# Joint softmax of the attention groups in steps between gate products, and branch values loaded into the places of two gate operands

## The chip, the cores and the metric

The kernel runs on 1 core of a Trainium2 chip. The metric is the device time of one execution in microseconds (us). Before the change the median of 3 runs is 1984.87 us, between 1984.15 and 1985.83.

## The reference

One layer of a hybrid decoder on 1024 tokens of width 1024, all in fp32. Cut to what matters here:

```
z = rms_norm(x) @ W_in          # one projection, its columns shared by all that follows
y_a = rwkv7_mixer(z_a)  @ proj_a     # branch A, 512 wide
y_b = rglru_mixer(z_b)  @ proj_b     # branch B, 512 wide
for each of 3 groups g (dilation 1, 4, 8):     # branch C: attention, 4 heads of 64 in a group
    logits = q_g @ k_g + bias;  m = max(logits);  p = exp(logits - m);  l = sum(p)
    o_g = (p @ v_g) / l;        lse_g = m + log(l)
w = softmax over the groups of lse           # the joint softmax
y_c = (sum_g w_g * o_g) @ proj_c             # 256 wide
gates = sigmoid(z_gate)                      # 3 branches x 1024 columns
merged = gates_a * y_a + gates_b * y_b + gates_c * y_c
x = x + merged @ W_out
x = x + relu(rms_norm(x) @ W_up)^2 @ W_down
```

## The kernel before

**Products.** Each fp32 product runs on TensorE (PE) as three matmuls of split operands, `mm3` (L236 to L238): high by high, high by low, low by high. The high part is a cast on ScalarE (ACT), the low part a subtraction on VectorE (DVE) or GpSimd (POOL). `load_w` does this for weights (`wr_` raw, `wh_` and `wl_` the parts, L225 to L229), `load_y` for branch values (`yr` raw, `y...h` and `y...l`, L336 to L343). Raw tiles of both, and those of the gate columns (`wr_z`, L1270), share a tag `wraw` with two places of 512 KB: a third raw load waits until the cast and the subtraction of one before it have freed its place.

**Stages.** Norm; the recurrent branch B, whose values go to DRAM as `yb_d`; branch A (RWKV, `ya_d`) with the attention's value, query and key projections in its gaps; the attention with the gate products as filler; `gates`, which multiplies the branch values with `proj_b`, `proj_a`, `proj_c` and sums them under the gates; `tail` with W_out and the MLP. The change touches the stretch from the attention to the start of `gates`.

**Gate products** (`gate_z`, L1205 on) are a generator: each `next` emits one step. The gate columns form 12 pairs of 128-column blocks, four for each of the branches B, C, A in this order. Pairs 0 and 1 are multiplied directly. Each of the other ten is made by seven half-size products, here called by their right operand in the order B11, B21, T2, T1, T3, B22, T4 (product j = 0 to 6): 12 matmuls each into one of two PSUM banks. B11 to B22 are the four quarters of the normed input (`ht`, shown as `hh` and `hl` in the profile, pool `hp`); T1 to T4 are sums of them in pool `h2`, shown as `zT1h` and so on (T4 takes the places of B12 in `hp`). The results that an add completes (`th`, L1334 on DVE) free a bank: in the order listings `th_103` is the add for pair 10, product 3. A tanh (L1258, ACT) and a store to `th_d` follow. The seven left operands of the next pair, `wz`, come from two raw tiles; for j = 2 they take four sums on DVE (`wr_z`, `th_s`, L1285 to L1289). In the last pair, pair 11, step j = 1 calls `load_first`: the first projection weights, `wr_p10`, and the four loads of branch B's values (`yr10` to `yr13`) into `wraw`. Their parts go to the places of T2 and T1 in `h2`.

**Attention** (L974 on) works in six units (cc, g): cc is the half of the four heads, g the group; the order is (0,0), (0,1), (0,2), (1,0), (1,1), (1,2), counted n = 0 to 5. A unit loads query and key (`z0`, `z1`), its bias tile and the row of key norms spread over partitions (`rb`, L121, a tag with two places), and DVE scales the key by it (`z`, L1001). Then four steps sp, with two `tiles` yields each: scores (`l`, L1018) into PSUM, their scaling (`lg`, L1028, DVE, which frees the scores' bank), max, exponential on ACT, transposes (`pt`), and the weighted values (`o`, L1063, copied to `og` at L1162). In the order listings `lg0130` belongs to group 0, cc 1, sp 3, and `z1_11` is the key of unit (1,1). After each yield `filler` draws gate steps from the generator: 71 of its 86 are drawn here, the rest run behind the attention.

**Joint softmax.** After a unit, `combine_rows` transposes its maxima and sums (`stt` on PE L1072, `st` on DVE L1074), stores them (`st_d`) and loads them back as rows of 16 x 128 (`row`, L1080). `combine(cc)` then does the joint softmax of the three groups: maxima (L1092), differences (L1096), exponentials on ACT, denominators (L1101, L1103), a reciprocal, the weights (L1106), which go to DRAM (`cw_d`) and come back spread over 64 partitions each (`cb`, L121), and the weighted sum `yc` = cb x og (L1122) plus the two `yt` (L1126), added on POOL and stored to `yc_d` (L1128). `combine(0)` runs on POOL and is called at once at sp = 2 of unit n = 3. `combine(1)` runs on DVE and is called at once after the last unit. In the order listings `mx1`, `ct1`, `row001`, `cw11`, `cw21` are its small tiles.

**Order.** A scheduler that simulates a timeline at build time places the instructions; the order of the program text is its priority, and `issue_after` keeps a filler step behind the scores of an earlier step. On the chip each engine runs its list in order. All loads and stores of this stretch are issued by SyncE (SP), also in order: one that must wait holds those behind it.

## Time and profile before

| | |
|---|---|
| median of 3 runs | 1984.87 us |
| profiled execution | 1979.91 us, its span 1978.1 us |
| mean granted clock of PE | 0.988 |
| PE busy | 1906.3 us, 96% of the span |
| PE weight loads (overlap PE) | 1512.1 us |
| DVE busy | 1237.5 us, 63% |
| ACT, POOL busy | 763.5 and 774.5 us, 39% each |
| moved by DMA | 236.53 MB, mean 120 GB/s |
| stretch 800 to 1085 us (most of the attention) | PE busy 278.74 of 285 us |
| stretch 1085 to 1182 us (end of the attention, last gate pairs, start of `gates`) | PE busy 80.17 of 97 us |
| stretch 1182 us to the end | PE busy 786.09 of 796 us |

The times of all rows are in us from the start of the span. L numbers are lines of the kernel. In a row of the timeline an arrow in brackets gives how long the engine had stood before the instruction and what ended that. Rows of stretches give, behind the limits and the length, the busy time (and count) of PE, its weight loads, DVE, ACT and POOL, then the granted clock of PE, the share of the DMA engines and the GB/s. PE is the engine that is nearly always busy, so what counts is the time in which it stands and what it waits for.

### The profile page before, as it was taken

Reading aid. Unit: us, or ns where it says so; the run is one execution under the profiler, and the core shown is the slowest. Engines: PE = TensorE matmul, PEld = TensorE weight load, DVE = VectorE, ACT = ScalarE, POOL = GpSimd, SP = SyncE. Lnnn points to the kernel's source line nnn. Section 1 sums busy time; section 2 is a strip of 40 time slices with the busy share of each in tenths; the row PEclk is TensorE's granted clock in tenths of the full one; section 3 lists DMA queues with packets and bytes.
Section 4 is the critical chain, followed back from the end, with each engine's and each line's share of the span. In section 5 each row is a group of like instructions: output and inputs, shape, how many; then the busy total and the mean of one; then the engine's idle time right before and its main releaser. Section 6 shows DMA issues by size and latency. Waiting matters only on the chain.

```text
span 1978.1 us, 29765 instructions
## 1 busy us (share of the span) xinstructions
PE 1906.3 (96%) x11634; PEld 1512.1 (76%) x11634; DVE 1237.5 (63%) x1992; ACT 763.5 (39%) x1275; POOL 774.5 (39%) x631
## 2 busy tenths in 40 slices
PE   8999999999999999999999879998999999999999
PEld 6776777787677878777777658887888888888887
DVE  5556456656656564775454446446777567987875
ACT  5675223233323331455555331245323323333332
POOL 1343533442452340542533442244343343444542
PEclk9999999999999999999999999999999999999999
DMA  4122312221221221434443465552433439535231
GB/s 147 54 65 75 98 46 62 59 57 50 54 71 40 66 65 38 131 99 149 120 145 111 150 236 183 188 181 107 160 138 149 165 137 380 196 144 181 95 128 65
DMA packets 191618, 236.53 MB, mean 120 GB/s; under 512 B 38536, under 2 KB 133413, under 8 KB 191478
## 3 DMA queue, kind: packets, MB, share of 16 engines
q1 hardware_dynamic: 191302, 234.62, 35.9%
q8 instruction: 91, 1.49, 0.3%
q14 instruction: 49, 0.40, 0.1%
q0 software_dynamic: 160, 0.02, 0.0%
q10 hardware_dynamic: 16, 0.00, 0.0%
HBM read 168.14 MB, written 68.82 MB: 120 GB/s over the span
## 4 chain that ended last, share of the span: by engine, by line
PE 77%; DVE 8%; DMA 6%; ACT 3%; issue 3%; POOL 3%; SPq 1%; DVEq 0%; ACTq 0%; POOLq 0%
PE dx L236 3%; PE dx L237 3%; PE dx L238 3%; PE zg L236 3%; PE ux L236 3%; PE ux L237 3%; PE ux L238 3%; PE zg L237 3%; PE zg L238 3%; PE g_z L237 2%; PE g_z L236 2%; PE g_z L238 2%; PE wo L238 1%; PE wo L236 1%; PE dz L237 1%
## 5 line engine op out<-in xcount | busy, mean ns | idle before, releaser
L1482 POOL TENSOR_TENSOR wl_d<-dr,wh_d 128x1024 fp32r<-128x1024 f32 x40 | 101.0, 2525 | 127.5 <-ACT wh_d L1481 119.0
L1291 POOL TENSOR_TENSOR wz<-wr_z,wz 128x512 fp32r<-128x512 f32 x60 | 84.0, 1401 | 162.9 <-ACT wz L1290 137.9
L1482 DVE TENSOR_TENSOR du<-dq,du 128x1024 fp32r<-128x1024 f32 x56 | 124.1, 2216 | 23.6 <-ACT du L1481 22.9
L236 PE MATMUL dx<-wh_d,du 128*128 128x512 f32 x256 | 99.7, 389 | 0.4 <-DVE acc L1662 0.4
L237 PE MATMUL dx<-wl_d,du 128*128 128x512 f32 x256 | 99.6, 389 | 0.0
L238 PE MATMUL dx<-wh_d,du 128*128 128x512 f32 x256 | 99.4, 389 | 0.0
L1481 ACT CAST wh_d<-dr 128x1024 fp32r<-128x1024 f32 x40 | 42.1, 1053 | 142.0 <-PE dx L238 72.8
L777 DVE TENSOR_SCALAR s<-ac,wc 64x64 f32<-64x64 f32 x128 | 36.1, 282 | 73.4 <-PE ac L773 71.0
L237 PE MATMUL g_z<-hl,wh_z 128*128 128x512 f32 x192 | 77.4, 403 | 0.0
L1482 POOL TENSOR_TENSOR wl_a<-ur,wh_a 128x1024 fp32r<-128x1024 f32 x15 | 47.6, 3175 | 75.7 <-ACT wh_a L1481 75.7
L236 PE MATMUL g_z<-hh,wh_z 128*128 128x512 f32 x192 | 76.6, 399 | 0.4 <-DVE zsq L432 0.4
L238 PE MATMUL g_z<-hh,wl_z 128*128 128x512 f32 x192 | 77.0, 401 | 0.0
L1482 POOL TENSOR_TENSOR wl_s<-ur,wh_s 128x1024 fp32r<-128x1024 f32 x16 | 44.4, 2774 | 76.0 <-ACT wh_s L1481 76.0
L229 POOL TENSOR_TENSOR wl_wo<-wr_wo,wh_wo 128x1024 fp32r<-128x1024 f32 x16 | 38.6, 2413 | 62.7 <-ACT wh_wo L228 62.7
L1481 ACT CAST du<-dq 128x1024 fp32r<-128x1024 f32 x56 | 58.6, 1047 | 1.5 <-DMA dq<-u_d 1.5
L1662 DVE TENSOR_TENSOR acc<-dx,acc 128x512 f32<-128x512 f32 x64 | 42.0, 680 | 26.3 <-PE dx L238 26.3
L236 PE MATMUL v<-wh_wv,hh 128*128 128x256 f32 x192 | 56.4, 294 | 1.3 <-DVE st L783 1.3
L236 PEld LDWEIGHTS dx<-wh_d,du 128*128 128x128 f32 x256 | 48.0, 188 | 10.9 <-DVE acc L1662 0.9
L237 PEld LDWEIGHTS dx<-wl_d,du 128*128 128x128 f32 x256 | 48.0, 188 | 10.0
L238 PEld LDWEIGHTS dx<-wh_d,du 128*128 128x128 f32 x256 | 48.0, 188 | 9.9
L237 PE MATMUL v<-wl_wv,hh 128*128 128x256 f32 x192 | 55.6, 290 | 0.0
L238 PE MATMUL v<-wh_wv,hl 128*128 128x256 f32 x192 | 55.3, 288 | 0.0
(757 smaller groups left out, 6160.6 us busy)
## 6 DMA issues: line engine op xcount, KB each, us to landing
dq<-u_d SPq DMA_DIRECT2D x56, 512.0 KB
wr_z<-in_w_in_dram SPq DMA_DIRECT2D x32, 512.0 KB
ur<-in_mlp_up_dram SPq DMA_DIRECT2D x16, 1024.0 KB
dr<-in_mlp_down_dram SPq DMA_DIRECT2D x16, 1024.0 KB
th_d<-th SPq DMA_DIRECT2D x48, 256.0 KB
tg<-th_d SPq DMA_DIRECT2D x32, 256.0 KB
wr_wo<-in_w_out_dram SPq DMA_DIRECT2D x16, 512.0 KB
qk_d<-zo SPq DMA_DIRECT2D x24, 256.0 KB
```

The lines of the kernel that those rows point to most:

```text
L229: E.tensor_tensor(lo, raw, hi, ALU.subtract)
L236: PE.matmul(ps, lh, rh, start=first and i == 0, stop=False, skip_group_check=skip)
L237: PE.matmul(ps, lh, rl, start=False, stop=False, skip_group_check=skip)
L238: end = PE.matmul(ps, ll, rh, start=False, stop=last and i == n - 1, skip_group_check=skip)
L777: V.tensor_scalar(ns[half[h], :], pb[h][half[h], 128 * j + 64 * c : 128 * j + 64 * c + 64], wc[half[h], 2 * i + c : 2 * i + c + 1], None, ...
L1291: (V if i == 2 else G).tensor_tensor(l, src, h, ALU.subtract)
L1481: A.copy(hi, src)
L1482: split.last = E.tensor_tensor(lo, src, hi, ALU.subtract)
L1662: V.tensor_tensor(acc[row][:, half[col]], ps, acc[row][:, half[col]], ALU.add)
```

## The change

Three things change.

1. `combine` becomes a generator with eleven yields: after the maxima, the exponentials, the denominators, the weights (two), and each of the six products with `og`. `combine(0)` starts at sp = 0 of unit n = 3 and takes two steps at each yield of the tiles that follow; what is left runs at the end of the unit. `combine(1)` still starts after the last unit, with one gate step drawn between its steps.
2. The raw values of branches B and A no longer pass through `wraw`. `raws` takes the places of B11 (for yb) and of B21 (for ya), high and low tile of each, as two tiles of 128 x 2 x 1024, and `load_first` issues the four loads of 1 MB: `yr1h` and `yr1l` hold rows 0 to 255 and 256 to 511 of `yb_d`, `yr0h` and `yr0l` those of `ya_d`. `load_y` with `raw` splits from there. The values of branch C (`yc`) still pass through `wraw`.
3. `load_first` is defined and handed over before `attention` is called, since more of the gate steps now run inside it, and the pool `yp` is opened behind the attention.

```
-    attention(..., fill)
...
-    def load_y(src, b, ks, place):
+    def load_y(src, b, ks, place, raw=None):
         for k in ks:
-            r = wp.tile([P, T], F32, tag="wraw", name=f"yr{b}{k}", bufs=2)
-            S.dma_start(r, src[k * P : (k + 1) * P, :])
+            r = (raw or (lambda k: wp.tile([P, T], F32, tag="wraw", name=f"yr{b}{k}", bufs=2)))(k)
+            if raw is None:
+                S.dma_start(r, src[k * P : (k + 1) * P, :])
             h, l = (place(k, x) for x in "hl")
             A.copy(h, r)
             (G if k % 2 else V).tensor_tensor(l, r, h, ALU.subtract)
...
+    def raws(b, kh):
+        t = []
+        for x in "hl":
+            r = hp.tile([P, 2, T], F32, tag=f"h{x}{kh}0", name=f"yr{b}{x}")
+            t += [r[:, 0], r[:, 1]]
+            S.dma_start(r, (yb_d if b else ya_d)[256 * "hl".index(x) : 256 * "hl".index(x) + 256, :].rearrange("(k p) t -> p k t", p=P))
+        return lambda k: t[k]
...
     def load_first():
         late.append(load_w(io["proj_b"][0][:, 0:256]...))
-        load_y(yb_d, 1, range(4), in_block(("T2", "T1"), 1))
+        late.extend((raws(1, 0), raws(0, 1)))
+        load_y(yb_d, 1, range(4), in_block(("T2", "T1"), 1), late[2])
     late.append(load_first)
+    attention(..., fill)
...
     def load_ya():
-        load_y(ya_d, 0, range(2), in_block(("T3",), 0))
-        load_y(ya_d, 0, range(2, 4), in_yp(0))
+        load_y(ya_d, 0, range(2), in_block(("T3",), 0), late[3])
+        load_y(ya_d, 0, range(2, 4), in_yp(0), late[3])
...
         def combine(cc):
...                                   # maxima
+            yield
...                                   # differences, exponentials
+            yield
...                                   # denominators, reciprocal
+            yield
...                                   # weights, cw_d, for cc = 1 the spread cb
+            yield
+            yield
             for hf in range(2):
                 for g, dil in enumerate(DILS):
...                                   # one product of cb and og
+                    yield
                 S.dma_start(yc_d[...], y)
...
+        sums = iter(())
...
                 for i, _ in enumerate(tiles(cc, g, sp, po)):
                     filler(0.2 if i else 2)
+                    next(sums, None)
+                    next(sums, None)
...
-                if sp == 2 and n == 3:
-                    combine(0)
+                if sp == 0 and n == 3:
+                    sums = combine(0)
+            for _ in sums:
+                pass
             combine_rows(cc, g)
-        combine(1)
+        for _ in combine(1):
+            filler(1)
```

**First place: DVE where unit (1,0) ends and the key of unit (1,1) is scaled.** `z1_11` waits for `rb`, the two `lg013` pairs free the scores of unit (1,0)'s last step, `th_6x` are gate adds. The rows carry each kernel's own line numbers: L1001, L1028 and L1334 became L1012, L1039 and L1357. Before:

```order
L1334 TENSOR_TENSOR th_63_9705<-zg60_9529,th_63_9705 128x512
L1001 SCALAR_TENSOR_TENSOR z1_11_9740<-z1_11_9740,der_111,rb110_9744 128x512
L1028 SCALAR_TENSOR_TENSOR lg0130_9660<-l0130_9654,sst_84,bias01_9237 128x256 x2
L1334 TENSOR_TENSOR th_62_9688<-zg61_9530,th_62_9688 128x512
L1001 SCALAR_TENSOR_TENSOR z1_11_9740<-z1_11_9740,der_111,rb111_9748 128x512
L1031 TENSOR_REDUCE stat01_9247<-lg0130_9660 128x2
L1028 SCALAR_TENSOR_TENSOR lg0131_9668<-l0131_9655,sst_84,bias01_9237 128x256 x2
```

After:

```order
L1039 SCALAR_TENSOR_TENSOR lg0131_9649<-l0131_9636,sst_84,bias01_9237 128x256 x2
L1309 TENSOR_TENSOR wr_z71_9574<-wr_z71_9574 128x512
L1042 TENSOR_REDUCE stat01_9247<-lg0131_9649 128x2
L1046 TENSOR_SCALAR nm0131_9650<-stat01_9247 128x2
L1311 TENSOR_TENSOR th_s7_9691<-wr_z70_9572,wr_z71_9574 128x512
L1312 TENSOR_TENSOR wr_z70_9572<-wr_z70_9572,th_s7_9691 128x512
L1314 TENSOR_TENSOR wz72_9688<-th_s7_9691,wz72_9688 128x512
L1357 TENSOR_TENSOR th_63_9686<-zg60_9553,th_63_9686 128x512
L1357 TENSOR_TENSOR th_62_9669<-zg61_9554,th_62_9669 128x512
L1012 SCALAR_TENSOR_TENSOR z1_11_9740<-z1_11_9740,der_111,rb110_9744 128x512
L1085 COPY st3201_9809<-stt01_9807 32x128
L1182 COPY og01_9318<-o013_9634 128x256
```

Both pairs of `lg013` now stand ahead of the two `z1_11` (that of `lg0130` five rows above the first row shown), and the gate adds `th_63` and `th_62` too; the `st` of unit (1,0) and a copy of the last `og01` come in between the first `z1_11` and the second, which is the row behind the last one shown.

**Second place: DVE behind the last `st`, with the arithmetic of `combine(1)` behind it.** Before, from the gate add that stands ahead of the arithmetic:

```order
L1334 TENSOR_TENSOR th_100_10670<-zg101_10657,th_100_10670 128x512
L1092 TENSOR_TENSOR mx1_10582<-mx1_10582,row201_10576 16x128
L1285 TENSOR_TENSOR wr_z110_10675<-wr_z111_10677,wr_z110_10675 128x512
L1096 TENSOR_TENSOR row001_9812<-row001_9812,mx1_10582 16x128
L1096 TENSOR_TENSOR cw11_10588<-row101_10258,mx1_10582 16x128
```

and from the last row of the arithmetic, fourteen rows further down:

```order
L1106 TENSOR_TENSOR cw21_10591<-cw21_10591,mx1_10582 16x128
L1334 TENSOR_TENSOR th_103_10726<-zg100_10656,th_103_10726 128x512
L1334 TENSOR_TENSOR th_102_10709<-zg101_10657,th_102_10709 128x512
L1122 TENSOR_TENSOR yc10_10615<-cb10_10602,og01_9318 128x512
L1126 TENSOR_TENSOR yt101_10617<-cb11_10607,og11_9818 128x512
L1126 TENSOR_TENSOR yt102_10620<-cb12_10612,og21_10264 128x512
L1126 TENSOR_TENSOR yt111_10626<-cb11_10607,og11_9818 128x512
L1126 TENSOR_TENSOR yt112_10629<-cb12_10612,og21_10264 128x512
L1334 TENSOR_TENSOR th_110_10804<-zg110_10790,th_110_10804 128x512
```

After, from the end of the arithmetic:

```order
L1120 TENSOR_TENSOR cw21_10609<-cw21_10609,mx1_10582 16x128
L1357 TENSOR_TENSOR th_100_10626<-zg101_10613,th_100_10626 128x512
L1308 TENSOR_TENSOR wr_z110_10631<-wr_z111_10633,wr_z110_10631 128x512
L1309 TENSOR_TENSOR wr_z111_10633<-wr_z111_10633 128x512
L1138 TENSOR_TENSOR yc10_10713<-cb10_10661,og01_9318 128x512
L1311 TENSOR_TENSOR th_s11_10708<-wr_z110_10631,wr_z111_10633 128x512
L1312 TENSOR_TENSOR wr_z110_10631<-wr_z110_10631,th_s11_10708 128x512
L1142 TENSOR_TENSOR yt101_10733<-cb11_10666,og11_9818 128x512
L1314 TENSOR_TENSOR wz112_10705<-th_s11_10708,wz112_10705 128x512
L1357 TENSOR_TENSOR th_103_10703<-zg100_10612,th_103_10703 128x512
L1142 TENSOR_TENSOR yt102_10754<-cb12_10671,og21_10264 128x512
L1142 TENSOR_TENSOR yt111_10797<-cb11_10666,og11_9818 128x512
```

Before, the add `th_100` stood ahead of the arithmetic and the sums for `wz112` were spread through it, with the four `yt` in one piece behind `th_102`. Now `th_100` and the four sums stand behind the arithmetic, and `th_103` and `th_102` between the products with `og`.

**Third place: SP around the loads of the branch values.** `wr_p10` and `wr_p00` are the first projection weights of branches B and A, `tb` the gate values that `gates` reads back. Before:

```order
L1259 DMA th_d_80<-th_103_10726 128x512
L1259 DMA th_d_80<-th_102_10709 128x512
L1259 DMA th_d_80<-th_106_10784 128x512
L225 DMA wr_p10_10824<-in_proj_b_dram 128x4x256
L1128 DMA yc_d_71<-yc10_10615 128x512
L340 DMA yr10_10830<-yb_d_70 128x1024
L1259 DMA th_d_80<-th_110_10804 128x512
L340 DMA yr11_10836<-yb_d_70 128x1024
L340 DMA yr12_10840<-yb_d_70 128x1024
L1128 DMA yc_d_71<-yc11_10624 128x512
L1259 DMA th_d_80<-th_113_10876 128x512
L1372 DMA tb100_10935<-th_d_80 128x512
```

After:

```order
L1282 DMA th_d_80<-th_103_10703 128x512
L1145 DMA yc_d_71<-yc10_10713 128x512
L1282 DMA th_d_80<-th_102_10686 128x512
L1282 DMA th_d_80<-th_106_10769 128x512
L360 DMA yr1l_10823<-yb_d_70 128x2x1024
L360 DMA yr1h_10821<-yb_d_70 128x2x1024
L225 DMA wr_p10_10815<-in_proj_b_dram 128x4x256
L1145 DMA yc_d_71<-yc11_10776 128x512
L360 DMA yr0l_10827<-ya_d_69 128x2x1024
L360 DMA yr0h_10825<-ya_d_69 128x2x1024
L225 DMA wr_p00_10995<-in_proj_a_dram 128x4x256
L1282 DMA th_d_80<-th_110_10792 128x512
```

The two loads of branch B's values stand ahead of its weights, and those of branch A follow ahead of every read of `tb`; the stores of `yc` keep their places on either side of branch B's loads.

More of the change, by code (lines that the diff above doesn't have):

```diff
@@ L330, in hybrid_block @@
     fill = gate_z(tc, w_in, ht, h2, hp, gt, wp, pg, th_d, load_cols, mm3, late)
-    attention(tc, io, dbg, psum, der, cg, yc_d, bias_d, sst, rk_d, cw_d, v_d, qk_d, fill)
-    yp_p = tc.tile_pool(name="yp", bufs=1)
-    yp = yp_p.__enter__()
     ys = {}
-    def load_y(src, b, ks, place):
+    def load_y(src, b, ks, place, raw=None):
         for k in ks:
-            r = wp.tile([P, T], F32, tag="wraw", name=f"yr{b}{k}", bufs=2)
-            S.dma_start(r, src[k * P : (k + 1) * P, :])
+            r = (raw or (lambda k: wp.tile([P, T], F32, tag="wraw", name=f"yr{b}{k}", bufs=2)))(k)
+            if raw is None:
+                S.dma_start(r, src[k * P : (k + 1) * P, :])
             h, l = (place(k, x) for x in "hl")
@@ L358, in load_first @@
         late.append(load_w(io["proj_b"][0][:, 0:256].rearrange("(k p) c -> p k c", p=P), [P, 4, 256], "p10"))
-        load_y(yb_d, 1, range(4), in_block(("T2", "T1"), 1))
+        late.extend((raws(1, 0), raws(0, 1)))
+        load_y(yb_d, 1, range(4), in_block(("T2", "T1"), 1), late[2])
     late.append(load_first)
+    attention(tc, io, dbg, psum, der, cg, yc_d, bias_d, sst, rk_d, cw_d, v_d, qk_d, fill)
+    yp_p = tc.tile_pool(name="yp", bufs=1)
+    yp = yp_p.__enter__()
     for _ in fill:
```

## The prediction

> **What bounds the kernel now.** I read the page first, then the waits of PE between 800 and 1260 us, then stretches of time, then the timelines of PE and DVE and the chain of waits where PE stood.
>
> ```profile
> span 1978.1 us, 29765 instructions
> PE 1906.3 (96%) x11634; PEld 1512.1 (76%) x11634; DVE 1237.5 (63%) x1992; ACT 763.5 (39%) x1275; POOL 774.5 (39%) x631
> ```
>
> PE is busy in 96% of the span and no matmul is removed, so only PE's own standing can be won: at most 72 us, most of it in stages that the change leaves alone. The waits of PE in the stretch that it touches (in total, times, longest):
>
> ```profile
> PE zg L236 <- DVE th L1334: 7.4, 3, 4.9
> PE l L1018 <- DVE lg L1028: 4.8, 3, 2.4
> PE pj L236 <- ACT y0T3h L342: 4.5, 1, 4.5
> PE pj L236 <- ACT y20h L342: 2.4, 1, 2.4
> PE pj L236 <- ACT wh_p L228: 1.4, 2, 1.0
> PE pj L237 <- POOL y1T1l L343: 1.3, 1, 1.3
> PE pj L237 <- DVE y20l L343: 0.5, 1, 0.5
> ```
>
> ```profile
> 1085.00:1182.00 97.00, 80.17 (x337) 61.79 (x334) 42.94 (x58) 32.60 (x48) 41.64 (x23) 0.96 0.58 188
> ```
>
> Between 1085 and 1182 us PE stands 16.8 us (97.00 less 80.17), and its granted clock is 0.96 there. PE's timeline places the waits for th and lg:
>
> ```profile
> 986.97 1.09 PE L1063 MATMUL o<-ptS,vt 128*64 128x128 f32 x16
> 1002.75 0.92 PE L1018 MATMUL l<-z,z 64*128 64x128 f32 x4 [2.45 <-DVE lg L1028]
> 1109.30 0.50 PE L236 MATMUL zg<-zT4h,wz 128*128 128x512 f32 x1 [1.76 <-DVE th L1334]
> 1112.18 0.39 PE L236 MATMUL zg<-hh,wz 128*128 128x512 f32 x1
> 1120.11 0.39 PE L238 MATMUL zg<-zT2h,wz 128*128 128x512 f32 x1
> 1125.40 0.79 PE L236 MATMUL zg<-zT1h,wz 128*128 128x512 f32 x1 [4.90 <-DVE th L1334]
> ```
>
> From 1112.18 to 1120.11 there are 36 matmuls, so one takes 7.93/35 = 0.227 us and a gate product of 12 takes 2.72.
>
> **The change part by part.** *Attention unit (1,1).* The wait of 2.45 is a queue on DVE:
>
> ```profile
> 1000.91 0.99 DVE L1001 SCALAR_TENSOR_TENSOR z<-z,der,rb 128x512 f32<-128x512 f32 x1 [5.32 <-DMA rb<-rk_d]
> 1001.83 0.86 DVE L1028 SCALAR_TENSOR_TENSOR lg<-l,sst,bias 128x256 f32<-128x256 f32 x2
> ```
>
> DVE stood 5.32 us for rb with the lg of the last tiles behind it, and those hold the score banks. In the new order (first place in the change section) both lg pairs stand ahead of that z. PE reaches the first scores of the unit after 57 gate matmuls from the o at 986.97 instead of 53, and eight pt, eight o and one stt more: 988.1 + 57 x 0.227 + about 2.3 (1.1 for the o by the row at 986.97, as much for the pt by estimate) is 1003.3. The z can be done by 1001.9, as now. So the 2.45 goes. Bounds: 0 gained if rb comes that much later (a bias load and a th_d store now stand ahead of it on SP), 2.45 if not; I take 2.45, since the z has over a microsecond to spare.
>
> *The joint softmax of the second half*, combine(1). DVE now:
>
> ```profile
> 1093.15 0.28 DVE L1074 COPY st<-stt 32x128 f32<-32x128 f32 x1 [5.86 <-PE stt L1072]
> 1093.73 0.43 DVE L1162 COPY og<-o 128x256 f32<-128x256 f32 x1 [0.30 <-PE o L1063]
> 1099.40 0.37 DVE L1092 TENSOR_TENSOR mx<-mx,row 16x128 f32<-16x128 f32 x1 [1.96 <-DMA row<-st_d]
> 1101.69 1.37 DVE L1101 TENSOR_TENSOR mx<-row,row 16x128 f32<-16x128 f32 x1
> 1102.99 0.38 DVE L1101 TENSOR_TENSOR ct<-cw,row 16x128 f32<-16x128 f32 x1
> 1104.08 0.67 DVE L1288 TENSOR_TENSOR th_s<-wr_z,wr_z 128x512 f32<-128x512 f32 x1
> 1106.35 0.62 DVE L1291 TENSOR_TENSOR wz<-th_s,wz 128x512 fp32r<-128x512 f32 x1
> 1106.89 1.35 DVE L1106 TENSOR_TENSOR row<-row,mx 16x128 f32<-16x128 f32 x1
> 1108.58 1.27 DVE L1334 TENSOR_TENSOR th<-zg,th 128x512 f32<-128x512 f32 x2
> 1117.14 1.10 DVE L1126 TENSOR_TENSOR yt<-cb,og 128x512 f32<-128x512 f32 x1 [1.70 <-DMA cb<-cw_d]
> 1124.67 0.68 DVE L1334 TENSOR_TENSOR th<-zg,th 128x512 f32<-128x512 f32 x1
> ```
>
> The th at 1108.58 and 1124.67 are the gate adds that free PE's banks. The first stood behind the row arithmetic, the last behind four yt, and PE waited 1.76 and 4.90 for them. In the new order (second place) the adds stand between the yt. These two waits go, and smaller ones come. Let S be the start of the last stt on PE, which now stands two products earlier in PE's order. From it PE has 48 gate matmuls, three o and the stt itself ahead of product T1 of pair 10: 10.9 + 0.8 = 11.7. T1 needs the add th_100, which now stands behind the row arithmetic: 0.3 to the st, 6.25 from st to row (1093.15 to 1099.40), then the arithmetic. That takes 9.2 now (1099.40 to 1108.58); four sums of 0.67 and a wz of 0.62 move behind it and one og of 0.43 comes in, so 6.3; with the add of 0.65, S+13.5. **New wait 1.8.** T4 of pair 10 is reached 36 matmuls later, at S+21.7; its add th_103 stands behind yc10 and yt101. The second cb was used 8.9 after the arithmetic's first result (1108.24 to 1117.14), here about S+21.1; with yt 1.1, wz 0.6 and the add, S+23.5. **New wait 1.8.** B11 of pair 11 then waits about 0.2 for th_102 behind two more yt. Bounds for each: 0 if the transfers come sooner, twice the value if one is as slow as the cb in the chain below; I take the middle, from the rows of the same steps.
>
> [...]
>
> *The branch values.* The chain of waits runs through the two wraw places, one load behind the other:
>
> ```profile
> 1112.75 6.40 DMA cb<-cw_d
> 1123.87 3.27 DMA yr<-yb_d
> 1138.95 5.79 DMA yr<-yb_d
> 1144.77 1.06 ACT y1T1h L342
> 1148.23 2.40 POOL wl_p L229
> 1150.65 4.46 DMA yr<-ya_d
> ```
>
> Load, cast, subtract, next load into the place that came free; the projections waited 4.5 + 2.4 + 1.4 + 1.3 + 0.5 = 10.1 for it. Now four loads of 1 MB need no wraw place, only the end of B11 and B21 of the last pair. With the waits above B11 ends at S+29.1. A load of 512 KB took 3.27; 512 KB more, at the 351 GB/s of the busiest slice, add 1.5:
>
> ```profile
> 1120.00:1130.00 10.00, 5.10 (x17) 3.79 (x16) 6.53 (x6) 3.34 (x5) 7.08 (x5) 0.83 0.44 153
> 1140.00:1150.00 10.00, 8.74 (x38) 6.80 (x38) 0.85 (x2) 2.89 (x4) 4.11 (x2) 1.00 0.99 351
> 1150.00:1160.00 10.00, 5.45 (x17) 3.75 (x17) 2.86 (x4) 2.34 (x3) 2.98 (x2) 0.83 0.68 246
> ```
>
> So yr1l lands at S+33.9 and yr1h, needed first, at S+36.9. Four casts of 1.06 follow on ACT, to S+41.1; behind them stands the copy th_113 (about 0.6, half a cast's elements), for which product B22, reached at S+40.0, has to wait. **New wait 1.7.** POOL does y1T2l, y1T1l and wl_p, 2.4 each, to about S+46.2; the last gate product ends at S+47.1, so the projections find their first operands ready. ya and its weights have 48 matmuls, 11 us, more, and yc 22. Bounds of what is left here: 0, and 4.5, the longest of these waits now, should the raw values be late; I take 1.7, by the loads that had the queue to themselves.
>
> *Clock.* In the slices at 0.83, 17 matmuls ran in 5.10 and 5.45 busy us where 22 and 24 fit at 0.227: 12 too few, 2.8 us. The new waits are well under the two, 4.90 and 4.5, that the clock fell behind, so this goes too.
>
> **Sum.** Gone: 2.45 + 1.76 + 4.90 + 10.1 + 2.8 = 22.0. New: 1.8 + 1.8 + 0.2 + 1.7 = 5.5. Gain 16.5. The profiled execution took 1979.91 (its span and 1.8 around it): 1963.4 after. The median of the runs, 1984.87, lies 4.96 above it; so **1968.4**, given as 1968.
>
> **The rivals.** *Nothing won in unit (1,1).* The steps of combine(0) leave POOL's rows nearly as they were, and since PE reaches the scores sooner, the wait for rb may only change its name. Then 2.45 stays: 1970.9.
>
> *The adds stay queued behind DVE's waits.* The arithmetic takes its old 9.2 with other sums inside, th_100 comes 2.9 later, the wait at T1 becomes 4.7 and costs about 1.2 of clock like the one of 4.90 did: 4.1 less, 1972.5. For it: DVE stands for the row with no gate add left ahead of that. Against: the sums that stretched the 9.2 are moved.
>
> *No new waits at all*: 1962.9.
>
> *The transfers bound.* 4 MB of raw values, 1 MB of weights and 2 MB of tb are 7 MB, and from 1088 to 1200 us the queues moved
>
> ```profile
> DMA packets 14039, 22.16 MB, mean 198 GB/s; under 512 B 1408, under 2 KB 7376, under 8 KB 14032
> ```
>
> At 198 GB/s yb is there at S+39.7 and B22 waits 4.5 rather than 1.7; the 7 MB are there at S+64 where ya is needed at S+58, 6 more, and 2 of clock: gain 6, 1979. Against it: the busiest slice moved 351 when loads were free to go.
>
> *Slower.* SP issues in order, and the big loads, the store of yc11 and the weights stand there one behind the other, each waiting for another engine. The store of yc11 hangs on four transfers (st_d, row, cw_d, cb) and on the store of yc10; it is due at about S+34, and ya and its weights stand behind it. Some 13 us of lateness are covered (ya is needed at S+58 and takes about 11 with its casts); beyond that each microsecond is PE's. To end 4 us slower than now it must come 13 + 16.5 + 4 = 34 us late: 1989 or more. No transfer in these rows is over 6.4.
>
> **How the numbers follow.** Forecast 0.56 (own range 1963 to 1974: no new waits to doubled ones), unit (1,1) unchanged 0.10, adds queued 0.13, no new waits 0.05, transfers 0.10, slower 0.06. A measurement of this kernel tells 0.2%, 4 us, from no change: 1980.9 to 1988.8 counts as the same. Faster: 0.56 + 0.10 + 0.13 + 0.05 and half of the transfers' case, 0.89; same: its other half, 0.05; slower 0.06. The range holds the first four and most of the transfers' case: 1961 to 1978.
>
> **What would show it.** In the new profile: no wait of PE for lg near 1000 us; waits for th of 1 to 3 us, at T1 and T4 of pair 10; all products of the last pair ahead of the first projection; the casts of yr1 starting 7 to 9 us behind the end of B11; a short wait at B22; no wait of the projections of 2 us; a granted clock of 1.00 in every slice behind 1100. I am wrong if PE stands over 10 us between the last scores and the second round of projections, if the casts of yr1 start at S+42 or later, or if waits appear in stages that the change leaves alone.

## The result and the profile after

The median went from 1985.83 us (seven runs, 1980.12 to 1993.63) to 1972.76 us (seven runs, 1969.19 to 1976.93), measured side by side: a ratio of 0.9932, interval 0.9911 to 0.9953, so 9 to 18 us are gained. The forecast was 1968, own range 1963 to 1974. The profiled executions differ by less: 1979.91 before, 1969.19 after. The heads of the page after:

```profile
span 1967.2 us, 29765 instructions
PE 1901.7 (97%) x11634; PEld 1511.0 (77%) x11634; DVE 1245.2 (63%) x1992; ACT 761.9 (39%) x1275; POOL 773.5 (39%) x631
```

To see where it went, two stretches of each trace: from the first scores to the first product of W_out, and the part of it behind the last `stt` (the tail). Before, then after:

```profile
815.36:1260.62 445.26, 422.17 (x2060) 320.10 (x2060) 258.00 (x472) 187.75 (x459) 176.51 (x120) 0.99 0.45 143
1092.83:1260.62 167.79, 150.96 (x645) 121.01 (x645) 94.76 (x125) 44.39 (x62) 60.91 (x30) 0.98 0.55 180
```

```profile
813.73:1249.34 435.61, 421.13 (x2059) 321.45 (x2059) 261.31 (x472) 186.15 (x459) 176.55 (x120) 0.99 0.45 146
1089.03:1249.34 160.31, 153.24 (x670) 125.07 (x667) 100.06 (x126) 45.73 (x67) 64.76 (x32) 0.99 0.56 192
```

The first scores come 1.6 us sooner (815.36 to 813.73), in code that the change leaves alone. The whole stretch is 9.65 shorter: PE stands 14.5 us in it (435.61 less 421.13) where it stood 23.1. What follows it takes 717.5 us before and 717.9 after. The tail after holds 24 gate matmuls more, because two products moved behind the last `stt`, as forecast; that is 24 x 0.227 = 5.45 us. With these counted where they were, the part ahead of the `stt` (the front) went from 277.5 to 280.8, **3.3 longer**, and the tail from 167.8 to 154.9, **12.9 shorter**.

The waits of PE from 800 to 1260 us in the profile after (in total, times, longest):

```profile
PE zg L236 <- DVE th L1357: 5.4, 4, 1.8
PE l L1029 <- DVE lg L1039: 3.9, 2, 2.7
PE zg L236 <- ACT th L1353: 2.4, 1, 2.4
...
```

No `pj` is left in the list; before, it had 10.1 us. Waits for `th` remain, and one of 2.7 for `lg`. PE's timeline places them:

```profile
1003.38 0.93 PE L1029 MATMUL l<-z,z 64*128 64x128 f32 x8 [0.76 <-DVE z L1012]
1016.84 0.43 PE L1074 MATMUL o<-ptS,vt 128*64 128x128 f32 x2 [0.44 <-ACT ptS L1067]
1021.62 1.65 PE L1029 MATMUL l<-z,z 64*128 64x128 f32 x4 [2.70 <-DVE lg L1039]
...
1102.14 0.50 PE L236 MATMUL zg<-zT1h,wz 128*128 128x512 f32 x1 [1.05 <-DVE th L1357]
1112.35 0.50 PE L236 MATMUL zg<-zT4h,wz 128*128 128x512 f32 x1 [1.76 <-DVE th L1357]
1117.19 0.50 PE L236 MATMUL zg<-hh,wz 128*128 128x512 f32 x1 [1.83 <-DVE th L1357]
1133.52 0.79 PE L236 MATMUL zg<-hh,wz 128*128 128x512 f32 x1 [2.43 <-ACT th L1353]
1134.11 0.63 PE L237 MATMUL zg<-hl,wz 128*128 128x512 f32 x1
...
1140.54 0.39 PE L236 MATMUL pj<-y1T2h,wh_p 128*128 128x512 f32 x1
```

The first three belong to unit (1,1), the next four are T1 and T4 of pair 10 and B11 and B22 of pair 11. The matmul at 1134.11 takes 0.63 where the last row has 0.39: the clock is down again behind the 2.43 (0.83 granted from 1130 to 1140 us). The first `pj`, at 1140.54, follows the last gate product without a gap.

DVE at the places of these waits:

```profile
1001.58 1.74 DVE L1012 SCALAR_TENSOR_TENSOR z<-z,der,rb 128x512 f32<-128x512 f32 x1 [3.81 <-DMA th_d<-th]
1006.83 0.75 DVE L1012 SCALAR_TENSOR_TENSOR z<-z,der,rb 128x512 f32<-128x512 f32 x1 [2.98 <-DMA rb<-rk_d]
...
1018.76 1.64 DVE L1308 TENSOR_TENSOR wr_z<-wr_z,wr_z 128x512 f32<-128x512 f32 x1 [5.72 <-DMA wr_z<-in_w_in_dram]
1021.10 0.47 DVE L1039 SCALAR_TENSOR_TENSOR lg<-l,sst,bias 128x256 f32<-128x256 f32 x1
...
1114.51 2.02 DVE L1142 TENSOR_TENSOR yt<-cb,og 128x512 f32<-128x512 f32 x2 [2.21 <-DMA cb<-cw_d]
1116.44 0.69 DVE L1357 TENSOR_TENSOR th<-zg,th 128x512 f32<-128x512 f32 x1
```

The first half of the scaled key, `z`, ended at 1003.32 (1001.58 + 1.74), and PE's 0.76 at 1003.38 is for it. (The bracket of that row names a store, the transfer that was inferred; what `z` reads is `rb`.) At 1018.76 DVE had stood 5.72 us for a raw tile of the gate columns, with the `lg` that free the score banks queued behind that sum. At 1114.51 it had stood 2.21 for a `cb`, with the add at 1116.44 behind two `yt`.

SP, which sends the loads of this place, after the change and then before (one spread is two transfers):

```profile
995.55 1.09 SPq L121 DMA_DIRECT2D cb<-cw_d  x2
997.78 1.08 SPq L121 DMA_DIRECT2D rb<-rk_d  x2
1003.35 1.72 SPq L121 DMA_DIRECT2D rb<-rk_d  x3
...
1012.97 0.54 SPq L1293 DMA_DIRECT2D wr_z<-in_w_in_dram  x1
```

```profile
997.38 2.62 SPq L121 DMA_DIRECT2D rb<-rk_d  x4
...
1007.28 3.98 SPq L1270 DMA_DIRECT2D wr_z<-in_w_in_dram  x2
```

Ahead of the first row SP now waits twice for 3.5 us, first for the place of a bias tile, then for that of the last `cb` of the first half, sent at 995.55; before, it waited 4.9 for a place ahead of the 997.38. The spread for the first half of `z` still goes out only 0.4 later than before (997.78 for 997.38), though the first scores came 1.6 sooner. The spread for the second half goes out at 1003.35, when DVE has ended the first half of `z`; before, both went out together. The raw columns of pair 8 come behind that: the second of their two loads leaves at 1012.97, before at 1010.89 (the second of the x2), and DVE's sum over them begins at 1018.76, before at 1014.85.

In the tail, three of SP's issues between 1105 and 1121:

```profile
1105.69 0.57 SPq L1121 DMA_DIRECT2D cw_d<-cw  x1
1109.91 1.09 SPq L121 DMA_DIRECT2D cb<-cw_d  x2
...
1120.43 0.46 SPq L360 DMA_DIRECT2D yr1h<-yb_d  x1
```

The last weights of the second half of the joint softmax are stored only at 1105.69, behind the spread of an earlier `cb`, and their own spread, begun at 1109.91, feeds the `yt` at 1114.51. The raw values that are needed first go out at 1120.43. ACT, which splits them:

```profile
1129.09 2.00 ACT L340 CAST y1T2h<-yr1h 128x1024 fp32r<-128x1024 f32 x2 [2.77 <-DMA yr1h<-yb_d]
1131.00 1.99 ACT L340 CAST y1T1h<-yr1l 128x1024 fp32r<-128x1024 f32 x2
1132.89 0.58 ACT L1353 COPY th<-zg 128x512 f32<-128x512 f32 x1
```

The copy that B22 needs stands behind the four casts, and PE waits 2.43 for it.

### The profile page after: what moved, and what is told of

The parts are those of the page before. It is cut to its first block, busy times and chain, and to the rows that moved or that the text cites. A ratio compares the mean times of both kernels' runs of the same rounds, so it can differ in the third digit from the quotient of the medians.

```text
span 1967.2 us, 29765 instructions
## 1 busy us (share of the span) xinstructions
PE 1901.7 (97%) x11634; PEld 1511.0 (77%) x11634; DVE 1245.2 (63%) x1992; ACT 761.9 (39%) x1275; POOL 773.5 (39%) x631
## 5 line engine op out<-in xcount | busy, mean ns | idle before, releaser
L1048 ACT ACTIVATE lg<-lg,nm 128x128 f32<-128x128 f32 (+1 forms) x96 | 42.3, 443 | 42.0 <-DVE nm L1046 42.0
L238 PEld LDWEIGHTS dx<-wh_d,du 128*128 128x128 f32 x256 | 48.1, 188 | 10.1
```

The lines of the kernel that those rows point to most:

```text
L238: end = PE.matmul(ps, ll, rh, start=False, stop=last and i == n - 1, skip_group_check=skip)
L1048: A.activation(lg[:, q, los[q] : 256], lg[:, q, los[q] : 256], AF.Exp, bias=nm[:, q : q + 1], accum_out=stat[:, 1, h, 2 * sp + q : 2 * sp ...
```

## The experiments

All kernels compute the whole reference. Diffs are against the changed kernel unless another is named. Ratios are to the kernel before, run beside them. Front and tail are the two parts of the stretch as above, from each profile, with the 24 moved matmuls (5.45 us) counted into the front where they run in the tail. They are of one execution each, so 2 or 3 us in them can be chance. By the ratios, no kernel of the table is told from the change with a gap between the intervals, except the kernel before and the one with the steps only:

| kernel | ratio | interval | front | tail |
|---|---|---|---|---|
| before | 1 | | 277.5 | 167.8 |
| the change | 0.9932 | 0.9911 to 0.9953 | 280.8 | 154.9 |
| raw values only | 0.9931 | 0.9907 to 0.9954 | 280.5 | 154.0 |
| steps only | 1.0002 | 0.9982 to 1.0022 | 284.3 | 167.3 |
| first half at once | 0.9933 | 0.9909 to 0.9958 | 280.8 | 153.8 |
| second half at once | 0.9939 | 0.9920 to 0.9958 | 282.4 | 157.3 |
| copy ahead of the casts | 0.9931 | 0.9909 to 0.9953 | 283.2 | 152.7 |
| adds ahead of the joint softmax | 0.9908 | 0.9876 to 0.9940 | 280.3 | 151.5 |
| adds and copy | 0.9885 | 0.9858 to 0.9911 | 280.8 | 148.3 |
| first half at once, z behind lg | 0.9890 | 0.9865 to 0.9915 | 277.4 | 152.1 |
| all of these | 0.9887 | 0.9862 to 0.9912 | 275.7 | 153.9 |
| still more adds ahead | 0.9928 | 0.9908 to 0.9947 | 275.1 | 159.1 |
| adds and copy, gate sum behind lg | 0.9887 | 0.9863 to 0.9911 | 276.9 | 148.4 |

### Which part brings the gain: raw values only, steps only

Raw values only:

```
-    next(sums, None)
-    next(sums, None)
...
-if sp == 0 and n == 3:
-    sums = combine(0)
-for _ in sums:
-    pass
+if sp == 2 and n == 3:
+    for _ in combine(0):
+        pass
...
 for _ in combine(1):
-    filler(1)
+    pass
```

> The kernel before with the third part of the change alone: the raw values of branches B and A in the places of B11 and B21; both joint softmaxes at once, as before. The prediction gave the raw loads 10.1 us and some of the 2.8 of clock, and the steps of the second half 2.9. Theory (the raw loads carry nearly the whole gain): from the last stt to the first product of W_out 155 to 159, where the kernel before had 167.8 and the kernel with the raw loads and the stepped second half 153.8; no wait of the projections over 1 us, waits for th of 5 to 8 as before; 0.992 to 0.996 of the kernel before. Rival (it takes the steps too, since the waits at the gates delay B11's end and so the loads): 160 or more, with waits of the projections, and 0.997 or more.

Steps only:

```
-late.extend((raws(1, 0), raws(0, 1)))
-load_y(yb_d, 1, range(4), in_block(("T2", "T1"), 1), late[2])
+load_y(yb_d, 1, range(4), in_block(("T2", "T1"), 1))
...
-load_y(ya_d, 0, ..., late[3])
+load_y(ya_d, 0, ...)
```

> The changed kernel, with the values of branches B and A loaded through the two wraw places again, all at the same place of the text; both joint softmaxes in steps. Theory (the two wraw places are what the projections waited for, 10.1 us in the kernel before, with 1.4 of clock behind the 4.55): the waits of the first round of projections come back to 8 to 12 us, the wait of 2.43 for the copy on ACT goes, and the span is 5 to 10 longer than the changed kernel's, so 0.996 to 1.000 of the kernel before. Rival (the waits went because the joint softmax no longer held SP's queue and the engines behind the gates): waits of the projections under 4 and a span within 2 of the changed kernel's.

The raw values alone gave 0.9931, the whole change 0.9932, the steps alone 1.0002. Waits of PE between 810 and 1260 us with the raw values alone, the two longest lines:

```profile
PE zg L236 <- DVE th L1354: 6.7, 2, 4.5
PE l L1029 <- DVE lg L1039: 5.7, 3, 2.4
```

and with the steps alone, whose lines for the projections come to 10.3 us with the six shorter ones:

```profile
PE zg L236 <- DVE th L1356: 4.4, 2, 2.3
PE pj L236 <- ACT y0T3h L340: 3.4, 1, 3.4
PE pj L236 <- ACT y20h L340: 2.4, 1, 2.4
```

So the projections' wait hangs on the raw values alone, and of the two parts run alone only they make the kernel measurably faster. The steps alone shorten the waits for `th` (7.4 before, 4.4 here), but that is paid back elsewhere: PE stands 22.8 us in the stretch, 23.1 before. The profiled execution of that kernel took 1995.22 us, 14 over its median, with PE busy 428.74 us in the stretch and not 422.17, so its front and tail in the table are too long.

The front with the raw values alone holds the code of before, and is 3.0 longer all the same:

```profile
812.27:1092.81 280.54, 274.04 (x1417) 201.13 (x1416) 163.04 (x347) 143.06 (x398) 114.96 (x90) 0.99 0.38 119
```

PE is busy 274.04 us in it, 271.21 before. So the 3.3 by which the change's front is longer can't, as a sum, be put down to the steps; the single waits can, where an experiment takes them away.

### The steps, one half at a time

First half at once, as before (the first two pieces of the diff above):

> The changed kernel, with the joint softmax of the first half called at once at sp = 2 of unit (1,0) again; the steps of the second half and the raw loads stay. In the changed kernel PE waited 0.76, 0.44 and 2.70 us in unit (1,1) and ran 1.4 us longer behind the 2.70 at the lower clock: 5.3 in all, where the kernel before had 2.45. Theory (the steps of the first half cost this: the load of the bias and the third cb then stand late on SP, rb and the raw gate columns of pair 8 behind them): the 2.45 for lg near 1000 us comes back, the waits near 1003 and 1021 go, and the span is about 2.9 shorter than the changed kernel's; 0.992 of the kernel before or less. Rival (chance of the execution, or the raw loads' part of the edit): the wait of 2 to 3 near 1021 stays, and the span stays within 1 of the changed kernel's. From the last stt on both expect no difference.

Second half at once (its last piece):

> The changed kernel, with the joint softmax of the second half at once behind the last unit again; the steps of the first half and the raw loads stay. Theory (my sum of the prediction: the steps of the second half take away the waits of 1.76 and 4.90 for th with 1.4 of clock behind the longer one, 8.1, and bring in 1.05 + 1.76 + 1.83 = 4.6): PE waits for th 6 to 7 us in all, one wait of 4 to 5, and the span is 3 to 4 longer than the changed kernel's. Rival (the raw loads alone carry the gain, since they free SP's queue and DVE of the work between): th waits of 4 us or less in all and a span within 1 of the changed kernel's. The waits in unit (1,1) are as in the changed kernel by both.

With the first half at once the ratio is 0.9933 and the span 0.7 shorter: its steps cost nothing net, against my theory of about 2.9. The waits for `lg` of 2.70 at 1021.62 went, as expected, so that wait does come from the steps of the first half. But 3.42 for `lg` stood at 1003 in its place, as this row of PE shows, and two waits for `th` came back, 1.98 and 4.51:

```profile
1003.12 0.92 PE L1029 MATMUL l<-z,z 64*128 64x128 f32 x4 [3.42 <-DVE lg L1039]
1004.52 0.63 PE L237 MATMUL zg<-hl,wz 128*128 128x512 f32 x1
```

The second of these is the surprise: the second half was still in steps. Without the first half's steps 156 gate matmuls run behind the last `stt`, not 180, so the four `yt` meet other products. The kernel with the raw values alone waits 2.16 and 4.49 at the same two, T4 of pair 10 and T1 of pair 11: with the first half at once, the steps of the second half change nothing here. With the second half at once the tail is 2.4 longer (waits for `th` of 1.07 and 3.90 on DVE and 2.08 on ACT); in the run with the profile the granted clock was also lower at places that neither theory names (0.97 over the stretch, 0.99 with the change; 0.83 from 820 to 830 us, 1.00 with the change), and the ratios can't tell it from the change. That one is inconclusive on the total.

### The new waits of the tail

The copy ahead of the casts: the split of yb, `late[1]`, is called at step j = 3 of the generator, behind the copy.

```
 if j in (0, 2, 3):
     t = tile(f"{n}{j}")
-    A.copy(t, bk)
+    copied = A.copy(t, bk)
...
+elif j == 3:
+    with tc.issue_after(copied.ins):
+        late[1]()
```

> The changed kernel, with the casts of branch B's values put behind the copy of product T1 of the last pair on ACT; their loads stay where they are. Theory (the 2.43 at B22 is that copy standing behind four casts of a microsecond): the wait at B22 goes, and the slow 7 matmuls behind it too, 3.8 in all; but the first projection then starts 3.8 earlier, and the low part of its weights, which POOL ended 0.2 before that product started, is 2 late: a new wait of the projections for POOL of 1.5 to 2.5, and a span 1 to 2.5 shorter than the changed kernel's. Rival (the bank is freed late by something else than the order on ACT): the wait at B22 stays over 1.5 and the span is as before within 1.

The adds ahead of the operations that held them up (th_100, th_103 and th_102 by the names of the order listings; `behind` keeps an instruction behind the add of that pair and product):

```
+            with behind(10, 1):
                 V.reciprocal(den, den)
...
+                        with behind(10, 4):
                             E.tensor_tensor(y, cb, ogs[(cc, 0)][:, sl], ALU.mult)
...
+                        with behind(10, 4 if hf == 0 and g == 1 else 5):
                             E.tensor_tensor(as_nat(t, g), as_nat(cb, g), ...)
...
-        for _ in combine(1):
-            filler(1)
+        filler(1)
+        for i, _ in enumerate(combine(1)):
+            filler(2 if i == 4 else 1)
```

> The changed kernel, with three gate adds of pair 10 put ahead of work that they stood behind on DVE: th_100 ahead of the reciprocal, th_103 ahead of the first product with og, th_102 ahead of the third; one gate step is drawn ahead of the joint softmax of the second half for that. Theory (the waits of 1.05, 1.76 and 1.83 at T1, T4 of pair 10 and B11 of pair 11 are DVE's order alone): all three are under 0.5, the stretch from the last stt to the first product of W_out, 160.3 in the changed kernel, is 4 to 5 shorter, and the casts of branch B's values start that much earlier too. Rival (the adds themselves wait for the cb transfers by the products that are moved, or the loads of branch B's values then come too late): other waits of 2 or more in their place, and the stretch within 1.5 of the changed kernel's.

Both together:

> The changed kernel with the adds of pair 10 ahead of the products with og and of the reciprocal, and with the casts of branch B's values behind the copy of T1 of the last pair. Theory: the waits for th (4.6) and the one at B22 with the slow matmuls behind it (3.8) go, 8.4 in all; the projections then want their operands 8 us earlier, while POOL ends the low parts only as much earlier as B11 ends, 4.6: a new wait of the projections of 2 to 4. The stretch from the last stt to W_out, 160.3, becomes 154 to 156; time 0.990 to 0.992 of the kernel before. Rival (the end of this stretch is set by the loads of the values, whatever the gates do): 158 to 160, with 5 or more of waits of the projections.

With the copy first the wait at B22 goes and the tail is 2.2 shorter; a new one of 1.9 for the low part of the weights stands at the projections. The ratio does not move, and the span is 3.0 longer, where 1 to 2.5 less was expected: the front of that profile is 2.4 longer, in code that this edit leaves alone. With the adds first the three waits at T1, T4 and B11 go and 0.8 stays at one product; the tail is 3.4 shorter, a little less than expected, because the copy now stands behind the cast of the first weights, which stood 4.44 us for its load, and behind two of the four casts, and B22 waits 3.26. Both together leave in 985 to 1145 us, besides 0.8 for z and 0.3 for an add:

```profile
PE l L1032 <- DVE lg L1042: 2.7, 1, 2.7
PE zg L237 <- ACT th L1361: 1.4, 1, 1.4
```

The tail is 6.6 shorter than with the change alone (160.31 to 153.74), and no projection waits, where 2 to 4 were expected. The 1.4 is at B22: the copy again stands behind the weight cast, which stood 4.50 for its load. So the causes named for the four waits are shown: those at T1, T4 and B11 went with DVE's order (one gate step is also drawn earlier in that edit), and the 2.43 at B22 with ACT's.

### Unit (1,1)

On the kernel with the first half at once, both scalings of the key are placed behind the last `lg` of the unit before:

```
+                with tc.issue_after(lgs_last[-1].ins) if (cc, g) == (1, 1) else nullcontext():
                     V.scalar_tensor_tensor(kn[:, sl], kn[:, sl], gcol, rb, ALU.mult, ALU.mult)
```

> The kernel with the joint softmax of the first half at once, in which PE waited 3.42 us for lg at the start of unit (1,1) and then ran 1.4 longer at the lower clock; here the two scalings of the key by rb are put behind the two lg pairs on DVE, and SP's order stays as in that kernel. Theory (what the prediction took for the 2.45: the lg stand behind a DVE instruction that waits for rb, and with that out of the way nothing is late): no wait over 1 us between 985 and 1045, 4 to 5 less than in that kernel. Rival (rb itself is what is late, and the scores of unit (1,1) then wait for the scaled key, or lg for the gate columns behind it): waits of 2 or more in that stretch under another name, and no more than 1.5 less.

Between 985 and 1045 us one wait is left, 1.52 for a gate add, where none over 1 was expected. The 3.42 is gone, and the stretch went from 434.60 to 429.52, 5.1 shorter, where 4 to 5 were expected; 3.4 of it are in the front, where the edit is. This is the wait that I forecast the steps themselves would remove.

On the kernel with adds and copy, the first sum over the raw tiles of pair 8 is placed behind the `lg` that it held up:

```
+            with tc.issue_after(LGS[-1].ins) if n == 8 else nullcontext():
                 V.tensor_tensor(a11, a21, a11, ALU.subtract)
```

> The kernel with the adds of pair 10 and the copy of T1 first (the third of the set of four, 429.1 us from the first scores to W_out), in which PE stood 2.70 near 1023 for an lg that stood on DVE behind the first sum of pair 8, which waited 5.7 in the changed kernel for the raw gate columns. Here that sum goes behind the second lg of the step. Theory: the 2.70 goes with the 0.8 to 1.4 of lower clock behind it, the 0.78 for the scaled key stays, product T2 of pair 8 finds its operand ready, and the stretch from the first scores to W_out is 425 to 426.5. Rival (PE waits for the sums instead, or the next scores for something else late by the same transfers): a wait of 1.5 or more under another name between 1015 and 1045, and 428 or more.

```profile
816.11:1241.41 425.30, 418.19 (x2060) 319.62 (x2059) 258.05 (x472) 186.18 (x459) 179.53 (x120) 1.00 0.46 150
```

The 2.70 is gone (0.99 remains, for the exponential behind the same scores, with matmuls of 0.63 behind it), and the stretch from first scores to W_out is 425.30, 3.8 less than with adds and copy. PE stands 7.1 us in it. Its median is 1959.73 against 1981.64 before, ratio 0.9887. This version beats the kernel before; its interval and that of the change (0.9863 to 0.9911, 0.9911 to 0.9953) only touch, though the two did not run side by side. It can't be told from adds and copy by the runs.

### Two that went past the mark

All of these: adds, copy and z behind `lg`, on the first half at once, with the split held behind the cast and the low part of wr_p10, the first weights.

```
-        load_y(yb_d, 1, range(4), in_block(("T2", "T1"), 1), late[3])
+        with tc.issue_after(late[5].ins), tc.issue_after(late[6].ins):
+            load_y(yb_d, 1, range(4), in_block(("T2", "T1"), 1), late[3])
```

> The kernel of the run before this one, with the joint softmax of the first half at once and the scaled key behind the lg pairs, as in the second run of this set. If both theories hold, it has 4 to 5 us less of waits in unit (1,1) than the changed kernel and 4 to 6 less behind the last stt: 0.988 to 0.990 of the kernel before. If unit (1,1) only changes the name of its wait, it comes out with the run before this one, 0.990 to 0.992.

Still more adds ahead, on that kernel:

```
-            with behind(10, 1):
+            with behind(10, 4):
                 V.reciprocal(den, den)
...
-                        with behind(10, 4):
+                        with behind(10, 5):
                             E.tensor_tensor(y, cb, ogs[(cc, 0)][:, sl], ALU.mult)
...
-                        with behind(10, 4 if hf == 0 and g == 1 else 5):
+                        with behind(*((11, 1) if hf else (10, 5))):
...
-            filler(2 if i == 4 else 1)
+            filler((2, 3)[i] if i < 2 else 1)
```

> The last kernel of the set before (joint softmax of the first half at once, scaled key behind the lg pairs, casts behind the copy of T1), in which PE still waited 1.91 at T4 of pair 10 and 3.10 at T1 of pair 11 for th and ran some 2.6 longer behind them at the lower clock. Here th_103 goes ahead of the reciprocal, th_102 ahead of the first product with og, and th_110 ahead of the products of the second half of tokens. Theory (DVE's order alone): both waits under 0.5, from the last stt to W_out 148 to 150 where that kernel had 153.9; 0.985 to 0.988 of the kernel before. Rival (the loads and casts of branch B's values, which only follow B11, or the weights' arithmetic made later, then bound the projections): waits of the projections of 2 or more and the stretch at 151 or more.

The first has the shorter front that its z gives, and loses it in the tail: T4 of pair 10 waits 1.91 and T1 of pair 11 waits 3.10. These are the two products at which each kernel with 156 gate matmuls behind the `stt` waits (before 1.76 and 4.90; z behind `lg` 1.80 and 2.85): the three adds were placed for the order with 180. The second, meant to mend that, made it worse. DVE there:

```profile
1122.41 1.03 DVE L1152 TENSOR_TENSOR yt<-cb,og 128x512 f32<-128x512 f32 x1 [2.34 <-DMA cb<-cw_d]
...
1163.23 6.23 DVE L1413 TENSOR_TENSOR tb<-tb,tg 128x512 f32<-128x512 f32 x3
```

The weights come later with the reciprocal, a `yt` waits for its `cb`, the next add stands behind that, and PE waits 4.73. Then three sums of `gates` took 2.08 each, and PE waited 3.89 more. A tail of 148 to 150 was expected, 159.1 was measured: the theory that every add can be put ahead failed. The row arithmetic has a due time of its own, since a transfer hangs on it. The edit also draws gate steps earlier, and no run separates the two.

## Why the prediction was right in sign and size, and where it failed

A gain of 16.5 us was forecast; the medians differ by 13.1, the profiled executions by 10.7. By its own terms, in the profiled executions:

| term | forecast | measured |
|---|---|---|
| unit (1,1) | 2.45 gone | 2.45 gone, 0.76 + 0.44 + 2.70 come |
| adds of before | 1.76 + 4.90 gone | gone |
| T1, T4, B11 | 1.8 + 1.8 + 0.2 come | 1.05 + 1.76 + 1.83 come |
| projections | 10.1 gone | gone |
| B22 | 1.7 comes | 2.43 comes |
| PE's standing, sum | 13.7 less | 8.2 less by these terms, 8.6 by the stretches |
| clock | 2.8 gone | PE busy 1.0 less |

**Unit (1,1): the step that failed.** "The z can be done by 1001.9, as now" held for neither half. The first half ran from 1001.58 and took 1.74 where it had taken 0.99, so it ended at 1003.32, and PE waited 0.76 for it. The second half ran from 1006.83, where it had run from 1003.21, because its spread left SP only when the first half was done. I had named the bias load as standing ahead of z and put the bound at no gain; that one late queue makes the next consumers late as well, the raw columns of pair 8 and then the `lg` behind DVE's sum, was in no bound. The bound needed a loss, 1.45. That the steps of the first half cause the 2.70, and DVE's queue carries it, is shown by the two experiments in which it went. With the first half at once SP sends both spreads together again, from 997.80, and DVE does not stand for those columns. Which of SP's stops makes them late is read from the rows; that kernel takes all of them away at once.

**Adds.** T1 and T4 were within 0.8 and 0.1 of the forecast, T1 by luck. With S at 1089.0, it began at S+13.1, forecast S+13.5, but two errors cancel in that:

```profile
1093.57 1.24 DVE L1103 TENSOR_TENSOR mx<-mx,row 16x128 f32<-16x128 f32 x1 [3.95 <-DMA row<-st_d]
1097.42 1.27 DVE L1116 TENSOR_TENSOR mx<-mx,ct 16x128 f32<-16x128 f32 x1
```

The row came at S+4.5, where S+6.55 was counted, and the arithmetic up to the add at 1101.41 took 7.84, where 6.3 was counted. One operation like these takes 0.27 to 0.38 elsewhere in the arithmetic. POOL made a `wz` beside each of the two (from 1093.30 and 1097.12) and beside the last two weights (1.57 together, POOL from 1099.82): three such places, where the 6.3 held two (the 1.37 and the 1.35 of before). So one more long place had a part in the 7.84, hidden by the early row. B11 was mis-sized, 1.83 for 0.2: the step "two more `yt`" counted their own time and not the third `cb`, whose store stood on SP behind an earlier spread.

**Raw values.** The casts began at S+40.1 for S+36.9: B11 ended 1.8 later by the waits above, and a load of 1 MB took 8.63 from issue to landing, beside its twin, where I had 7.8. The wait at B22 is then the forecast one, with its queue, and 0.7 longer. The projections' 10.1 went whole, the largest term, and the one on which the sign rested. On POOL, though, the cover was thin:

```profile
1136.91 3.40 POOL L229 TENSOR_TENSOR wl_p<-wr_p,wh_p 128x1024 fp32r<-128x1024 f32 x1
```

It is the last of three parts, which took 2.4, 3.4 and 3.4 where I counted 2.4 each; it ended at 1140.31, 0.23 ahead of the first `pj`. The kernel with the copy first ran into just this.

**Clock.** "The new waits are well under the two, so this goes too" failed. A granted clock of 1.00 in every slice behind 1100 was named as the mark, and 1130 to 1140 has 0.83; a second place stands behind the 2.70:

```profile
1020.00:1030.00 10.00, 8.38 (x28) 6.24 (x29) 7.99 (x22) 5.46 (x20) 0.43 (x1) 0.66 0.00 1
1130.00:1140.00 10.00, 7.57 (x27) 5.81 (x26) 9.07 (x6) 9.98 (x13) 8.83 (x3) 0.83 1.04 402
```

By the stretches, PE's busy time fell 3.2 in the tail (153.24 less 5.45 against 150.96) and rose 2.1 in the front, where the granted clock was 1.00 before; with the raw values alone it rose 2.8 there, so the 2.1 can't be put down to the steps.

**The rivals.** "Nothing won in unit (1,1)" came nearest, and reality went past it. "The adds stay queued" did not happen: T1 waited 1.05 and not 4.7. "The transfers bound" did not: the last row has 402 GB/s, over twice the 198 of that case, and no projection waits. "No new waits" fell with the four waits above. Nor did the slower case happen: the store of yc11 was out by 1124.43, S+35.4, with ya behind it in 1 us.

**The attribution** was wrong though the sum was near. I gave the steps 2.45 + 6.66 less 3.8 for their new waits, and part of the clock, some 6.7 in all; run alone they are worth nothing that can be measured. I gave the raw values the rest, some 9.8; run alone they bring a ratio of 0.9931, some 14 us. One part was taken 6.7 too high and the other some 4 too low, and the range was met partly by luck: for the raw values the mechanism was right, for the steps it was not, since most of what they took away came back at another product or in unit (1,1).

## What to carry to other kernels

When a stage is broken into steps, its DMA issues spread over the in-order queue as well (here the second spread of `rb` left 5.6 us behind the first, 1003.35 for 997.78, and the columns of pair 8 behind it): list for each what then stands behind it, and follow the late load to its consumer, and to what is queued behind that consumer. Moving work off a queue paid here where a wait hung on a place that is recycled (two places for all raw tiles, 10.1 us); spreading it over gaps brought nothing here by itself, and PE's waits went where the instructions that free its banks were placed by hand ahead of those that wait. No run has such placing without any steps, so what the steps add to it is open. After each such move look again at which products the late operations fall on: a shift of two gate products brought back waits that had been removed, twice here.

## What the hardware showed that was not expected

**The clock fell behind short waits too, and not behind each.** PE's slow matmuls start 0.427 us apart and not 0.227 (granted clock 0.50 from 1023 to 1026 us after the change), for some 3 us or twice that; seven such matmuls cost 1.4 us. They followed waits of 2.43 and 2.70 after the change and of 3.42 with the first half at once; none followed the 2.45 before at the same place. The same wait of 1.15 us near 824 us, in code that no kernel here changed, has both. First the window and a row of the kernel with z behind `lg`, then the kernel with adds and copy:

```profile
820.00:830.00 10.00, 8.85 (x33) 6.70 (x32) 10.00 (x17) 4.12 (x8) 4.67 (x3) 0.83 0.32 110
...
824.36 1.78 PE L1030 MATMUL l<-z,z 64*128 64x256 f32 x8 [1.15 <-DVE lg L1040]
826.55 0.63 PE L237 MATMUL zg<-hl,wh_zg 128*128 128x512 f32 x1
```

```profile
820.00:830.00 10.00, 8.15 (x36) 5.91 (x34) 10.00 (x17) 4.13 (x8) 4.70 (x3) 1.00 0.37 118
...
824.33 1.78 PE L1032 MATMUL l<-z,z 64*128 64x256 f32 x8 [1.15 <-DVE lg L1042]
826.37 0.40 PE L238 MATMUL zg<-hl,wh_zg 128*128 128x512 f32 x1
```

So in these runs a wait of 1 to 3 us cost its own length and nothing on top (1.05, 1.76 and 1.83 after the change, 2.45 before) or 1.4 us or more on top (2.43 and 2.70 after the change), and no row foretells which. Its length alone does not decide it, as the 1.15 shows, nor does the form of the matmuls around it: slow matmuls followed a gap of 2.43 with full gate products on both sides, and one of 1.15 with the scores behind it, which are 64*128 in the row and not 128*128.

**DVE's sums varied threefold.** A `tb` sum of 0.68 took 2.08 in the row at 1163.23 above while POOL made the low parts of two weights (from 1163.28 to 1168.91), and PE waited 3.89 behind them. The 1.24 and 1.27 of the row arithmetic look alike: each ended 0.1 to 0.2 us behind a `wz` of POOL (1.28 from 1093.30 and 1.44 from 1097.12). Nothing had been moved at the `tb` sums but the times at which the two engines met. No run takes POOL's work away, so that it lengthens DVE's is read from these rows and not shown.
